# First batch's x through SP's hardware queue as fp32, in place of a casting load issued by POOL

## The chip, the cores and the metric

One core of one Trainium2 chip. The metric is the device time of one launch in microseconds (us). Runs are sorted into fast and slow by their time and by the clock that PE was granted.

Engines: PE multiplies matrices, DVE and ACT copy from PSUM (where PE leaves its results) to SBUF (where its operands lie), POOL and SP issue DMAs here. Sixteen DMA engines move the data between HBM, the memory outside the core, and SBUF. What POOL issues stands in the profile as the software queue, what SP issues as the hardware queue.

## The reference

```python
batch, m, k, n = 32, 512, 1024, 768
x      = randn(batch, m, k)  float32
weight = randn(batch, k, n)  float32
return np.matmul(x, weight)  # float32
```

A batch reads 2.10 MB of x and 3.15 MB of w and writes 1.57 MB of output, all as fp32 in HBM; 32 batches are 218 MB.

## The kernel before

Loads are issued by POOL and cast fp32 to bf16 on the way. PE transposes x as pairs of bf16 viewed as fp32 (so one fp32 transpose moves two bf16 columns), DVE copies the result out of PSUM, PE multiplies in bf16, ACT and DVE copy the sums to SBUF, and POOL issues the store.

```python
def load_x(b):
    xs[b] = x_pool.tile([P, MT, K], BF16, name="x_sb")
    nc.gpsimd.dma_start(out=xs[b], in_=x_view[b])       # POOL, casts

def load_w(b):
    ws[b] = w_pool.tile([P, KT, N], BF16, name="w_sb")
    ...                                                  # POOL, casts

def transpose(b, mt):
    pt = tpsum.tile([P, JT, P], F32, name="pt")
    pairs = xs[b].bitcast(F32)
    for j in range(JT):                                  # 4 transposes
        nc.tensor.transpose(pt[:, j, :], pairs[:, mt, j::JT], ident)
    xT = xT_pool.tile([P, JT, P, 2], BF16, name="xT")
    nc.vector.tensor_copy(...)                           # 1 copy
    return xT

load_x(0)
load_w(0)
ident = ...
for b in range(1, AHEAD):        # AHEAD = 3; x and w have 4 buffers each
    load_x(b)
    load_w(b)
for b in range(B):
    if b + AHEAD < B:
        load_x(b + AHEAD)
        load_w(b + AHEAD)
    if b > 0:
        nc.gpsimd.dma_start(out=out_view[b - 1], in_=outs[b - 1])
    ...                          # transposes, matmuls, evacuation
```

Of the kernel before, what the change touches and what calls it, by code (L numbers as in the profile page):

```python
# [1 line left out]

# [5 lines left out]

F32 = mybir.dt.float32
BF16 = mybir.dt.bfloat16  # L10


@with_exitstack
def kernel(
    ctx: ExitStack,
    tc: tile.TileContext,
    x: bass.AP,
    weight: bass.AP,
    out: bass.AP,
):  # L20
    nc = tc.nc
    B, M, K = x.shape
    _, _, N = weight.shape
    P = 128
    MT = M // P
    KT = K // P
    JT = KT // 2
    N2 = 2 * N
    CHUNKED = {B - 4: (4, 4), B - 3: (4, 4), B - 2: (4, 4), B - 1: (4, 2, 2)}
    AHEAD = 3  # L30

    const = ctx.enter_context(tc.tile_pool(name="const", bufs=1))
    w_pool = ctx.enter_context(tc.tile_pool(name="w", bufs=4))
    x_pool = ctx.enter_context(tc.tile_pool(name="x", bufs=4))
    xT_pool = ctx.enter_context(tc.tile_pool(name="xT", bufs=8))
    out_pool = ctx.enter_context(tc.tile_pool(name="out", bufs=7))
    tpsum = ctx.enter_context(tc.tile_pool(name="tpsum", bufs=2, space=bass.MemoryType.PSUM))
    mpsum = ctx.enter_context(tc.tile_pool(name="mpsum", bufs=2, space=bass.MemoryType.PSUM))



    w_view = weight.rearrange("b (ki ko) n -> b ki ko n", ki=P)
    x_view = x.rearrange("b (mi mo) k -> b mi mo k", mi=P)
    out_view = out.rearrange("b (mi mo) n -> b mi (mo n)", mi=P)

    xs, ws, outs = {}, {}, {}

    def banks():
        return [mpsum.tile([P, 512], F32, name=f"pm{i}") for i in range(3)]

    def load_x(b):
        xs[b] = x_pool.tile([P, MT, K], BF16, name="x_sb")
        nc.gpsimd.dma_start(out=xs[b], in_=x_view[b])  # L53

    def load_w(b):
        ws[b] = w_pool.tile([P, KT, N], BF16, name="w_sb")
        at = 0
        for n in CHUNKED.get(b, (KT,)):
            nc.gpsimd.dma_start(out=ws[b][:, at:at + n, :], in_=w_view[b, :, at:at + n, :])  # L59
            at += n  # L60
# [5 lines that stand above are left out]
        for j in range(JT):  # L66
            nc.tensor.transpose(pt[:, j, :], pairs[:, mt, j::JT], ident)  # L67
        xT = xT_pool.tile([P, JT, P, 2], BF16, name="xT")
        nc.vector.tensor_copy(  # L69
            xT.rearrange("p j m r -> p (j m r)"), pt.bitcast(BF16).rearrange("p j m -> p (j m)")  # L70
        )
        return xT



    SPLITS = (
        ((0, 0, 0, 512), (1, 0, 512, N - 512)),
        ((1, N - 512, 0, 1024 - N), (2, 0, 1024 - N, N2 - 1024)),
    )

    def matmuls(pm, half, xT, b, kos, together):
        for ko in kos:
            for i, (bank, at, off, size) in enumerate(SPLITS[half]):
                shares = half == 1 and i == 0
                nc.tensor.matmul(  # L85
                    pm[bank][:, at:at + size],
                    xT[:, ko // 2, :, ko % 2],
                    ws[b][:, ko, off:off + size],
                    start=(ko == 0 and not (together and shares)),
                    stop=(ko == KT - 1),  # L90
                    skip_group_check=together,
                )

    def evacuate(b, pair, pm):
        o = outs[b][:, pair * N2:(pair + 1) * N2]
        nc.scalar.copy(o[:, 0:512], pm[0])  # L96
        nc.vector.tensor_copy(o[:, 512:1024], pm[1])  # L97
        nc.scalar.copy(o[:, 1024:N2], pm[2])  # L98

    with tc.manual_schedule():  # L100
        load_x(0)
        load_w(0)
        ident = const.tile([P, P], F32)
        make_identity(nc, ident)
        for b in range(1, AHEAD):
            load_x(b)
            load_w(b)

        ready = {}
# [5 lines that stand above are left out]
                nc.gpsimd.dma_start(out=out_view[b - 1], in_=outs[b - 1])  # L115
            outs[b] = out_pool.tile([P, MT * N], F32, name="out_sb")
            if b not in CHUNKED:
                xT = {mt: transpose(b, mt) for mt in (0, 1)}
                for pair in range(2):
                    pm = banks()  # L120
                    for half in range(2):
                        if pair == 0:
                            matmuls(pm, half, xT[half], b, range(KT), False)
                            xT[2 + half] = transpose(b, 2 + half)
                        else:
                            matmuls(pm, half, xT[2 + half], b, range(KT), False)
                    evacuate(b, pair, pm)
                continue
            xT = ready.pop(b, None) or {mt: transpose(b, mt) for mt in range(MT)}
            pms = [banks() for _ in range(2)]  # L130
            at = 0
            for n in CHUNKED[b]:
                last = at + n == KT
                for mt in range(MT):
                    if last and b + 1 < B:
                        ready.setdefault(b + 1, {})[mt] = transpose(b + 1, mt)
                    matmuls(pms[mt // 2], mt % 2, xT[mt], b, range(at, at + n), True)
                    if last and mt % 2 == 1:
                        pair = mt // 2
                        evacuate(b, pair, pms[pair])  # L140
                        if b == B - 1:
                            cols = slice(pair * N2, (pair + 1) * N2)
                            nc.sync.dma_start(out_view[b, :, cols], outs[b][:, cols])
                at += n


# [1 line left out]
_INS = ['x', 'weight']  # L148
_OUTS = [((32, 512, 768), 'float32')]


# [23 lines left out]
```

## Time and profile before

| | before |
|---|---|
| time, first three runs, median | 518.48 us |
| span of the profiled execution | 516.5 us |
| PE, DVE, ACT busy | 82%, 25%, 15% |
| software DMA queue busy, of 16 engines' span | 99.9% |

The page of the kernel before: DMA busy tenths in 40 slices of the span, then the queues with packets, MB and busy share.

```profile
DMA  8999999999999999999999999999999999999996
q0 software_dynamic: 14400, 132.65, 99.9%
q1 hardware_dynamic: 288, 1.57, 0.7%
```

Only the first and the last of the 40 slices are not full (a 9 stands for 90% or more). What is to be saved in DMA time without moving fewer bytes lies, for the most part, there.

The timeline of POOL in the kernel before (start, length, engine, line, operation, output and input; in brackets the idle time ahead and what ended it), first the head, then one batch of the steady part:

```profile
1.26 0.67 POOL L53 DMA_DIRECT2D x_sb<-in_x_dram  x1 [0.81 <-POOLq L159]
1.93 0.55 POOL L59 DMA_DIRECT2D w_sb<-in_weight_dram  x1
...
25.44 0.53 POOL L53 DMA_DIRECT2D x_sb<-in_x_dram  x1 [19.23 <-PE pt L67]
30.64 0.53 POOL L59 DMA_DIRECT2D w_sb<-in_weight_dram  x1 [4.67 <-PE pm L85]
...
321.69 0.53 POOL L53 DMA_DIRECT2D x_sb<-in_x_dram  x1 [6.69 <-DMA w_sb<-in_weight_dram]
325.36 0.53 POOL L59 DMA_DIRECT2D w_sb<-in_weight_dram  x1 [3.14 <-DMA out_dram<-out_sb]
330.26 0.54 POOL L115 DMA_DIRECT2D out_dram<-out_sb  x1 [4.38 <-DMA x_sb<-in_x_dram]
337.47 0.53 POOL L53 DMA_DIRECT2D x_sb<-in_x_dram  x1 [6.67 <-DMA w_sb<-in_weight_dram]
```

In the steady part each issue waits until an earlier transfer has landed (the one eight places before), so the gaps between issues are the durations of transfers: an output lands 3.67 us after a w, an x 4.90 us after that, a w 7.21 us later. That is 428 to 436 GB/s each, counted in fp32 bytes, although x and w are written to SBUF as half as many bf16 bytes. A batch takes 15.78 us of DMA.

The timeline of PE in the kernel before, its first transposes and first matmuls, and two pieces of the chain that ended last (start, length, what), around the landing of the last x:

```profile
9.55 1.96 PE L67 MATMUL pt<-ident,x_sb 128*128 128x128 f32 x8 [9.55 <-DMA x_sb<-in_x_dram]
16.70 4.89 PE L85 MATMUL pm<-w_sb,xT 128*128 128x512 bf16 x16 [5.19 <-DMA w_sb<-in_weight_dram]
```

```profile
457.72 31.16 DMA x_sb<-in_x_dram
488.88 0.04 issue
```

### The profile page before, as it was taken

How to read it: one execution, taken by the hardware profiler on the slowest of the kernel's cores; microseconds unless marked ns; L12 is line 12 of the kernel's file. 1: busy time of each engine (PE TensorE's matmuls, PEld its weight loads, DVE VectorE, ACT ScalarE, POOL GpSimd, SP SyncE). 2: the span in 40 equal slices, each digit the busy share in tenths (PEclk: the TensorE clock that was granted, in tenths of full speed). 3: DMA queues.
4: the chain of work that ended last, by engine and by line, in shares of the span. 5: the costliest groups of instructions: out<-in, count | busy, mean ns of one | idle time of the engine just before them, and what ended most of it. 6: DMA issues, size and time to landing. Idle time of an engine off the chain costs nothing.

```text
span 516.5 us, 5888 instructions
## 1 busy us (share of the span) xinstructions
PE 424.2 (82%) x2512; PEld 277.7 (54%) x2560; DVE 127.0 (25%) x192; ACT 76.3 (15%) x129; POOL 53.9 (10%) x106
## 2 busy tenths in 40 slices
PE   1799999788887979868897879887887986978992
PEld 1466666455554656545564546554555653655561
DVE  1133333133131331322321213312223121322221
ACT  0011111111111111101110101111111110111111
POOL 3011010100101001100011010010100101111000
PEclk9999999899897998989998979998899897988997
DMA  8999999999999999999999999999999999999996
GB/s 158 217 218 216 211 274 278 272 268 240 263 274 275 278 249 246 279 275 274 266 233 270 278 275 271 245 256 278 273 276 255 245 273 272 276 266 242 256 387 265
DMA packets 14714, 134.60 MB, mean 261 GB/s; under 512 B 1632, under 2 KB 1632, under 8 KB 3040
## 3 DMA queue, kind: packets, MB, share of 16 engines
q0 software_dynamic: 14400, 132.65, 99.9%
q1 hardware_dynamic: 288, 1.57, 0.7%
q8 instruction: 20, 0.33, 0.2%
q14 instruction: 6, 0.05, 0.0%
HBM read 167.77 MB, written 50.33 MB: 422 GB/s over the span
## 4 chain that ended last, share of the span: by engine, by line
DMA 74%; PE 21%; DVE 2%; issue 1%; ACT 0%; POOL 0%; POOLq 0%
DMA w_sb<-in_weight_dram 37%; DMA out_dram<-out_sb 24%; PE pm L85 19%; DMA x_sb<-in_x_dram 13%; PE pt L67 2%; DVE xT L69 1%; DVE out_sb L97 1%; ACT out_sb L98 0%; POOL x_sb L53 0%; POOLq L53 0%; POOLq L59 0%; POOLq L159 0%
## 5 line engine op out<-in xcount | busy, mean ns | idle before, releaser
L85 PE MATMUL pm<-w_sb,xT 128*128 128x256 bf16 (+1 forms) x2000 | 370.7, 340 | 66.6 <-DMA w_sb<-in_weight_dram 61.9
L85 PEld LDWEIGHTS <-xT 128*128 128x128 bf16 x2048 | 207.2, 102 | 204.6 <-issue 72.9
L69 DVE COPY xT<-pt 128x1024 bf16<-128x1024 bf16 x128 | 85.8, 689 | 264.0 <-PE pt L67 264.0
L67 PE MATMUL pt<-ident,x_sb 128*128 128x128 f32 x512 | 80.3, 291 | 15.9 <-DMA x_sb<-in_x_dram 15.6
L67 PEld LDWEIGHTS pt<-ident,x_sb 128*128 128x128 f32 x512 | 76.3, 207 | 24.1 <-issue 14.6
L96 ACT COPY out_sb<-pm 128x512 f32<-128x512 f32 x64 | 37.5, 586 | 287.9 <-PE pm L85 284.5
L97 DVE COPY out_sb<-pm 128x512 f32<-128x512 f32 x64 | 43.9, 687 | 116.2 <-PE pm L85 116.2
L98 ACT COPY out_sb<-pm 128x512 f32<-128x512 f32 x64 | 37.5, 586 | 142.4 <-PE pm L85 142.2
L53 POOL DMA_DIRECT2D x_sb<-in_x_dram x32 | 17.1, 536 | 192.6 <-DMA w_sb<-in_weight_dram 141.8
L59 POOL DMA_DIRECT2D w_sb<-in_weight_dram x37 | 19.7, 532 | 114.2 <-DMA out_dram<-out_sb 56.5
L115 POOL DMA_DIRECT2D out_dram<-out_sb x31 | 16.6, 536 | 136.8 <-DMA x_sb<-in_x_dram 64.7
L96 ACT ACT_TABLE_LOAD x1 | 1.3, 1283 | 0.7 <-PEq L159 0.7
masks.py:199 POOL TENSOR_SCALAR_AFFINE_SELECT ident<-ident 128x128 f32<-128x128 f32 x1 | 0.3, 288 | 0.1
masks.py:197 POOL MEMSET ident<- 128x128 f32 x1 | 0.2, 243 | 0.0
L159 POOL MEMSET const-float32-0.0<- 128x1 f32 x1 | 0.1, 99 | 0.2 <-issue 0.2
L159 POOL MEMSET const-bfloat16-1.0<- 128x1 bf16 x1 | 0.1, 103 | 0.0
L159 POOL MEMSET const-uint8-127<- 128x1 uint8 x1 | 0.1, 103 | 0.0
L159 POOL MEMSET const-float32-1.0<- 128x1 f32 x1 | 0.1, 100 | 0.0
## 6 DMA issues: line engine op xcount, KB each, us to landing
out_dram<-out_sb POOLq DMA_DIRECT2D x31, 1536.0 KB, 41.9
w_sb<-in_weight_dram POOLq DMA_DIRECT2D x28, 1536.0 KB, 43.2
x_sb<-in_x_dram POOLq DMA_DIRECT2D x32, 1024.0 KB, 39.6
w_sb<-in_weight_dram POOLq DMA_DIRECT2D x7, 768.0 KB, 31.4
out_dram<-out_sb SPq DMA_DIRECT2D x2, 768.0 KB, 7.0
w_sb<-in_weight_dram POOLq DMA_DIRECT2D x2, 384.0 KB, 28.7
```

The lines of the kernel that those rows point to most:

```text
L53: nc.gpsimd.dma_start(out=xs[b], in_=x_view[b])
L59: nc.gpsimd.dma_start(out=ws[b][:, at:at + n, :], in_=w_view[b, :, at:at + n, :])
L67: nc.tensor.transpose(pt[:, j, :], pairs[:, mt, j::JT], ident)
L69: nc.vector.tensor_copy(xT.rearrange("p j m r -> p (j m r)"), pt.bitcast(BF16).rearrange("p j m -> p (j m)"))
L85: nc.tensor.matmul(pm[bank][:, at:at + size], xT[:, ko // 2, :, ko % 2], ws[b][:, ko, off:off + size], start=(ko == 0 and not (together an ...
L96: nc.scalar.copy(o[:, 0:512], pm[0])
L97: nc.vector.tensor_copy(o[:, 512:1024], pm[1])
L98: nc.scalar.copy(o[:, 1024:N2], pm[2])
L115: nc.gpsimd.dma_start(out=out_view[b - 1], in_=outs[b - 1])
L159: nc = _bacc.Bacc("TRN2", target_bir_lowering=False, num_devices=1)
```

## The change

The intent: SP stands idle at the start and can issue before POOL does. SP's load is written as a plain copy, so x of batch 0 arrives as fp32; each of its four row groups then needs eight fp32 transposes in place of four paired ones, and two DVE copies that also round to bf16.

```diff
+    first_pool = ctx.enter_context(tc.tile_pool(name="first", bufs=1))
...
+    def transpose_first(mt):
+        xT = xT_pool.tile([P, JT, P, 2], BF16, name="xT")
+        for h in range(2):
+            pt = tpsum.tile([P, JT, P], F32, name="pt")
+            for i in range(JT):
+                nc.tensor.transpose(pt[:, i, :], x_first[:, mt, JT * h + i::KT], ident)
+            nc.vector.tensor_copy(
+                xT[:, 2 * h:2 * h + 2].rearrange("p j m r -> p j r m"),
+                pt.rearrange("p (j r) m -> p j r m", r=2),
+            )
+        return xT
...
-        load_x(0)
+        x_first = first_pool.tile([P, MT, K], F32)
+        nc.sync.dma_start(x_first, x_view[0])
         load_w(0)
...
-                xT = {mt: transpose(b, mt) for mt in (0, 1)}
+                turn = transpose if b else lambda _, mt: transpose_first(mt)
+                xT = {mt: turn(b, mt) for mt in (0, 1)}
...
-                            xT[2 + half] = transpose(b, 2 + half)
+                            xT[2 + half] = turn(b, 2 + half)
```

## The prediction

> What bounds the kernel now. The DMA engines. The page's slices show DMA at 0.9 or more in all but the first and last, and its queue line shows the software queue busy 99.9% of the engines' span; PE is 82% busy, DVE 25%. After 86 us the chain of waits is almost all DMA. Before that it is PE, but with slack: eight loads (21 MB read) are queued by 6 us, and PE takes 12.8 us a batch against 15.8 us of DMA.
>
> What a transfer costs. In POOL's timeline, from about 59 us on, each issue follows the landing of the transfer eight places before, so the gaps between issues measure transfers: x 4.92 us, w 7.2, output 3.66, 15.8 a batch. Over the fp32 bytes (2.10, 3.15, 1.57 MB) all are 426 to 437 GB/s. The time goes with the fp32 side, not with the bf16 side that a cast writes. So x of batch 0 costs the same 4.9 us when written as fp32: the change takes no DMA work away and adds none.
>
> What it moves. POOL issues its first DMA at 1.26 us (0.67 us long); the first packet is recorded near 2.65 us. SP is free from 0.7 us. In the tail SP issued at 506.06 us and its first packets appear about 0.9 us later. My estimate from these: SP's first packets near 1.7 to 1.9 us, so the engines start 0.7 to 0.9 us earlier. The Trainium skill, "DMA: Bandwidth & Descriptors", section "Issuing engines are not separate DMA queues", says that all queues share the same 16 engines and a second issuer only saves issue time; the equal rates here fit. What is saved at the head moves the whole saturated queue, with it the landing of the last x (488.9 us) and the end. That is the whole gain: about 0.8 us of 518.
>
> What it adds, off the critical path. x and w of batch 0 share the engines: together still 5.24 MB, so w lands near 16 us (16.66 before), but x at about 14 us in place of 9.5. Sixteen fp32 transposes (245 ns each in the cold first group) and four copies of about 0.69 us (as the 128x512 fp32 eviction) then precede the matmuls: first matmul 17 to 18.5 us, before 16.70. Batch 0 has 16 more transposes (160 ns each, 2.6 us of PE) and 4 more DVE copies (2.8 us). PE is 2 to 4 us late with batch 0. It costs nothing: POOL's refills at 30.6 to 44 us come that much later, while the queued 21 MB last until about 50 us; the x load of batch 4 no longer waits for batch 0's transposes (issued near 6 us, was 25.4).
>
> Predicted time: 517.7 us, 516.7 to 518.6 in 8 of 10. Faster by over 2%: 0.01; within 2%: 0.98; slower: 0.01.
>
> What would show the steps right: first packets before 2 us on the hardware queue; x of batch 0 landing at 13 to 15.5 us; w within 1 us of 16.6; the x load of batch 4 issued by 7 us; POOL's steady gaps unchanged; the last x landing 0.5 to 1 us earlier; the tail after it still about 28 us.
>
> What would make it wrong: SP issuing no earlier than POOL (gain 0); the two queues disturbing each other so that the first 5.24 MB take longer than 12 us; a PE delay over 20 us that drains the queue; an order of issues that leaves the last loads later; a clock change in the tail, which is matmul-bound.

## More of the kernel before

The head in windows (length, then busy time of PE, its weight loads, DVE, ACT and POOL, then PE's granted clock, the DMA engines' busy share, GB/s written), kernel before:

```profile
0.00:2.00 2.00, 0.00 (x0) 0.00 (x0) 0.00 (x0) 1.25 (x1) 0.94 (x6) 1.00 0.00 0
2.00:4.00 2.00, 0.00 (x0) 0.00 (x0) 0.00 (x0) 0.03 (x1) 1.92 (x5) 1.00 0.83 86
```

And the DMA view of the first 20 us: all packets, then the software queue.

```profile
DMA packets 401, 3.55 MB, mean 177 GB/s; under 512 B 32, under 2 KB 32, under 8 KB 32
q0 software_dynamic: 401, 3.55, 88.9%
```

No byte moves in the first 2 us. These 3.55 MB are bf16, so 7.10 MB of fp32 were read; this sum, "fp32 MB by 20 us", is the measure of the head used below. At 430 GB/s 7.10 MB would take 16.5 us, so by this estimate about 3.5 us of the head go unused.

## The result

| | before | after |
|---|---|---|
| time, median of 6 runs each | 518.13 us | 517.64 us |
| range | 517.75 to 518.51 | 516.90 to 517.73 |
| ratio of the fast runs, 95% interval | | 0.9987, 0.9975 to 1.0 |
| span of the profiled execution | 516.5 us | 516.0 us |
| fp32 MB by 20 us | 7.10 | 7.56 |
| w of batch 0 landed | 16.63 us | 15.87 us |

A ratio is the mean time of one kernel's fast runs over the mean of the other's in the same rounds, so it is not quite the ratio of the medians.

The page of the changed kernel, its queues:

```profile
q0 software_dynamic: 14256, 131.60, 98.9%
q1 hardware_dynamic: 432, 3.67, 1.9%
```

The first 20 us of the changed kernel, DMA view:

```profile
DMA packets 434, 4.83 MB, mean 241 GB/s; under 512 B 41, under 2 KB 41, under 8 KB 41
q0 software_dynamic: 290, 2.73, 64.9%
q1 hardware_dynamic: 144, 2.10, 29.0%
```

The 2.10 MB on the hardware queue are fp32 as written; the 2.73 MB on the software queue stand for 5.46 MB. Together 7.56 MB, 0.46 MB more than before at the same moment. At 430 GB/s that is a lead of 1.07 us. (The page's own GB/s must not be used for this: it counts written bytes, and it rises merely because x is now written as fp32.)

The head of the changed kernel, windows:

```profile
0.00:2.00 2.00, 0.00 (x0) 0.00 (x0) 0.00 (x0) 1.26 (x1) 0.94 (x6) 1.00 0.46 90
2.00:4.00 2.00, 0.00 (x0) 0.00 (x0) 0.00 (x0) 0.02 (x1) 1.93 (x5) 1.00 0.63 205
```

The engines now work before 2 us, though they are not full yet (share 0.63 from 2 to 4 us); SP's first packets stand in the window from 1.6 to 1.8 us, where before the first was recorded at 2.6 to 2.7 us. The timeline of the changed kernel:

```profile
0.74 0.38 SPq L116 DMA_DIRECT2D x_first<-in_x_dram  x1
1.26 0.67 POOL L60 DMA_DIRECT2D w_sb<-in_weight_dram  x1 [0.81 <-POOLq L175]
...
5.61 0.59 POOL L54 DMA_DIRECT2D x_sb<-in_x_dram  x1
12.38 3.60 PE L81 MATMUL pt<-ident,x_first 128*128 128x128 f32 x16 [12.38 <-DMA x_first<-in_x_dram]
15.87 2.76 PE L99 MATMUL pm<-w_sb,xT 128*128 128x512 bf16 x16
...
28.51 0.53 POOL L60 DMA_DIRECT2D w_sb<-in_weight_dram  x1 [22.31 <-PE pm L99]
```

SP issues at 0.74 us and its x lands 11.5 us later, at 12.24. The x load of batch 4 is out at 5.61 us, 20 us earlier than before, but only behind seven others in a full queue. The refill of w comes at 28.51 us, 2.1 us earlier than before. In the chain the last x lands here, hardly moved:

```profile
457.90 31.18 DMA x_sb<-in_x_dram
489.08 0.04 issue
```

So the head gained 0.76 us (landing of w) to 1.07 us (bytes), this profiled execution is 0.5 us shorter, and yet the last x landed 0.20 us later than before. A single pair of traces does not close the account; the experiments do.

### The profile page after: what moved, and what is told of

Same layout as the page of the kernel before. It is cut to its first block, busy times and chain, and to the rows that moved or that the text cites. A ratio compares the mean times of both kernels' runs of the same rounds, so it can differ in the third digit from the quotient of the medians.

```text
span 516.0 us, 5924 instructions
## 1 busy us (share of the span) xinstructions
PE 426.4 (83%) x2528; PEld 279.6 (54%) x2576; DVE 129.7 (25%) x196; ACT 76.3 (15%) x129; POOL 53.4 (10%) x105
## 4 chain that ended last, share of the span: by engine, by line
DMA 88%; PE 9%; issue 1%; DVE 0%; ACT 0%; POOLq 0%
DMA x_sb<-in_x_dram 37%; DMA w_sb<-in_weight_dram 25%; DMA out_dram<-out_sb 24%; PE pm L99 7%; DMA x_first<-in_x_dram 2%; PE pt L81 1%; PE pt L68 1%; DVE out_sb L111 0%; DVE xT L70 0%; ACT out_sb L112 0%; POOLq L130 0%; POOLq L54 0%; POOLq L60 0%
## 5 line engine op out<-in xcount | busy, mean ns | idle before, releaser
L70 DVE COPY xT<-pt 128x1024 bf16<-128x1024 bf16 x124 | 83.0, 689 | 245.4 <-PE pt L68 245.4
L68 PE MATMUL pt<-ident,x_sb 128*128 128x128 f32 x496 | 77.4, 290 | 8.9 <-DMA x_sb<-in_x_dram 8.6
L68 PEld LDWEIGHTS pt<-ident,x_sb 128*128 128x128 f32 x496 | 73.7, 207 | 17.2 <-issue 7.1
L130 POOL DMA_DIRECT2D out_dram<-out_sb x31 | 16.6, 536 | 140.8 <-DMA x_sb<-in_x_dram 62.8
L81 PE MATMUL pt<-ident,x_first 128*128 128x128 f32 x32 | 5.7, 338 | 12.4 <-DMA x_first<-in_x_dram 12.4
L81 PEld LDWEIGHTS pt<-ident,x_first 128*128 128x128 f32 x32 | 4.9, 202 | 13.0 <-issue 12.3
L82 DVE CAST xT<-pt 128x512 bf16<-128x512 f32 x8 | 5.5, 727 | 18.4 <-PE pt L81 18.3
## 6 DMA issues: line engine op xcount, KB each, us to landing
x_first<-in_x_dram SPq DMA_DIRECT2D x1, 2048.0 KB, 11.5
```

The lines of the kernel that those rows point to most:

```text
L70: nc.vector.tensor_copy(xT.rearrange("p j m r -> p (j m r)"), pt.bitcast(BF16).rearrange("p j m -> p (j m)"))
L81: nc.tensor.transpose(pt[:, i, :], x_first[:, mt, JT * h + i::KT], ident)
L82: nc.vector.tensor_copy(xT[:, 2 * h:2 * h + 2].rearrange("p j m r -> p j r m"), pt.rearrange("p (j r) m -> p j r m", r=2),)
```

## The experiments

Theory A is the prediction's: the engines start about 0.8 us earlier, and because they are full from there to the end, that lead reaches the end. Its rivals: B, batch 0 is computed earlier, which frees buffers earlier; C, the half microsecond is scatter; D, a plain copy on the hardware queue is cheaper than a cast on the software queue. Each result gives the median, and the ratio to the kernel before with its 95% interval. Calls of several kernels shared one chip and nine runs of before.

### The change again, twice (no edit)

> The changed kernel unedited, for a second profile and more timed pairs. Theory A (the engines start earlier and the saturated queue carries that to the end): ratio to before 0.998 to 0.9995, w of batch 0 lands at 15.6 to 16.1 us (before 16.63, first profile of the change 15.87), about 0.4 to 0.5 MB (in fp32 bytes) more moved by 20 us than before. Theory C (the half microsecond is run to run scatter): ratio 1.000 within 0.001 and the head's lead no larger than what two profiles of one kernel differ by.

> The changed kernel unedited once more, beside the three below, so that they are compared with it on one chip. Theory A: ratio to before 0.9980 to 0.9993 as in the first two measurements (0.9987, 0.9993).

First repeat: 517.49 us, ratio 0.9993 (0.998 to 1.0005). Second: 517.00 us, ratio 0.9976 (0.9963 to 0.9988). The gains of the three measurements, as differences of means, are 0.65, 0.43 and 1.33 us; their average is 0.81 us. With the first repeat alone C would stand; the interval of the second excludes it. That ratio of 0.9976 lies below the range expected (0.9980 to 0.9993).

The head repeats itself closely: fp32 MB by 20 us are 7.62 and 7.56, w of batch 0 lands at 15.7 to 15.8 us. The last x landed at 488.2 us in both, 0.67 us before the profiled execution of before. The chain of the first repeat:

```profile
457.04 31.17 DMA x_sb<-in_x_dram
488.21 0.04 issue
```

The first profile of the change was thus an unlucky one, and that of before a lucky one, as the kernels of the experiments below show. In the four traces without an early start the last x landed at 488.88 (before), 489.25 (before with the tail edit), 489.23 (POOL's fp32 load) and 489.68 us (SP held back), on average 489.26. In the six with one, and POOL on time, it landed at 489.08, 488.21 and 488.22 (the change), 488.82 (batch 1), 487.88 and 488.50 us (both with the tail edit), on average 488.45: the lead is still 0.81 us at the last load. The times say the same: 31 runs of those with an early start average 517.35 us, 48 of those without 518.27, which is 0.92 us, with a standard error of 0.1. That excludes C.

Where the single traces part can be placed: POOL's steady issues are equally spaced again in all of them from about 160 us on, but for steps near 220 to 250 us and at 442 us, and the 0.9 us between the first profile of the change and its repeat arise between 60 and 115 us, where POOL's waits pass from PE to the DMAs. Why is open.

### SP's load held back

```diff
-        nc.sync.dma_start(x_first, x_view[0])
         load_w(0)
+        nc.gpsimd.memset(x_first[:, 0, 0:1], 0.0)   # SP must wait for this
+        nc.sync.dma_start(x_first, x_view[0])
```

> Only the start of SP's load is held back, behind a small write on POOL that follows the issue of w of batch 0; fp32 load, hardware queue, transposes and casts stay. Theory A: the lead is gone, first packet near 2.6 us from the software queue as before, w of batch 0 and x together done near 16.6 us, time 518.0 to 518.6, ratio 0.999 to 1.001. Theory D (a plain copy on the hardware queue is cheaper for the engines than a cast on the software queue): the lead stays, ratio about 0.9987 as in the change.

518.45 us, ratio 1.0008 (0.9994 to 1.0022): no gain is left, with the rest of the change in place but for the order (w of batch 0 is now issued first). The interval overlaps that of the change on the same chip (0.998 to 1.0005), so the lead in bytes decides, and it is gone. D falls: fp32, hardware queue and all, it is no cheaper. So does another rival, that POOL, with one load fewer, issues the rest one place earlier: here too it does (w of batch 0 at 1.26 us, before 1.93). DMA view of the first 20 us, this kernel:

```profile
q0 software_dynamic: 259, 2.52, 64.2%
q1 hardware_dynamic: 144, 2.10, 25.0%
```

2.10 MB and twice 2.52 MB are 7.14 MB; the kernel before has 7.10 and the change 7.56. The expectation missed one thing: x and w were not done together near 16.6 us. w landed at 15.2 and x only at 18.8 us. The timeline of this kernel:

```profile
2.07 0.38 SPq L118 DMA_DIRECT2D x_first<-in_x_dram  x1
...
18.90 3.50 PE L81 MATMUL pt<-ident,x_first 128*128 128x128 f32 x16 [18.90 <-DMA x_first<-in_x_dram]
22.24 2.76 PE L99 MATMUL pm<-w_sb,xT 128*128 128x512 bf16 x16
```

PE began its matmuls 5.5 us later than in the kernel before, and the time is 0.3 us above it, which the interval does not tell from nothing. So PE has slack of that order in the head. (That batch 0 came late is not what took the gain: with the early load of batch 1, below, it comes late too and the gain stays.)

### The fp32 load issued by POOL

```diff
-        nc.sync.dma_start(x_first, x_view[0])
+        nc.gpsimd.dma_start(out=x_first, in_=x_view[0])
```

> x of batch 0 is still loaded as fp32 and transposed as fp32, but issued by POOL at the place of the old load. Theory A: no lead; x lands near 9.5 us, w near 16.6 us, ratio 0.999 to 1.001. Theory D with the cast as the cheaper or dearer part: x lands more than 0.3 us earlier or later than the 9.5 us of before. Also: PE will sit idle about 3 us between the transposes and the first matmul; if the idle gap is what made the first 16 matmuls take 4.9 us in before and 2.8 us after the change, they take more than 2.8 us here.

518.24 us, ratio 1.0005 (0.9993 to 1.0018). x landed 8.1 us after its issue (8.2 with the cast, before), w at 16.66 us. fp32 MB by 20 us: 7.10, as before. A plain copy and a cast of the same fp32 source took the engines the same time. The gain belongs to SP's early issue, not to the type.

PE then waited for w, and this kernel's timeline shows what that costs:

```profile
16.66 4.19 PE L99 MATMUL pm<-w_sb,xT 128*128 128x512 bf16 x16 [3.50 <-DMA w_sb<-in_weight_dram]
```

The first 16 matmuls took 4.19 us after 3.50 us of idle time, 4.89 us after 5.19 us in the kernel before, and 2.76 us in the first two traces of the change, where the transposes run straight into them. In the second repeat, though, they took longer without any gap:

```profile
16.01 3.84 PE L99 MATMUL pm<-w_sb,xT 128*128 128x512 bf16 x16
```

Over all traces the first sixteen took 2.76 to 3.84 us without a gap and 4.19 to 5.28 us behind one of 3.5 us or more. This kernel has the same sixteen transposes as the change, so the gap is the likely cause that the matmuls behind it are slow; the 3.84 us show that it is not the only one. (In the kernel before only eight transposes precede the gap; that PE had not come up to speed there is possible too.)

### Another batch's x through SP

SP loads x of batch 1 at the start; batch 0 is loaded by POOL as before.

```diff
-        nc.sync.dma_start(x_first, x_view[0])
+        nc.sync.dma_start(x_first, x_view[1])
+        load_x(0)
...
-            load_x(b)
+            if b > 1:
+                load_x(b)
...
-                turn = transpose if b else lambda _, mt: transpose_first(mt)
+                turn = transpose if b != 1 else lambda _, mt: transpose_first(mt)
```

> SP loads x of batch 1 as fp32 at the start, in place of batch 0's; batch 0 is loaded by POOL with a cast as in before. Theory A: any bytes moved early count, so the lead in fp32 bytes by 20 us and the time are those of the change (ratio 0.998 to 0.9995), though x and w of batch 0 land 3 to 5 us later (w near 20 us) and PE starts later. Theory B (the gain is that batch 0 is computed earlier, which frees buffers and starts the refills earlier): no gain or a loss.

516.99 us, ratio 0.9980 (0.9968 to 0.9993), no slower than the change. x of batch 0 landed at 13.6 us and w at 20.8 us, both over 4 us later than before the change, so batch 0 was late. B falls: what batch the early bytes belong to does not matter, only that they move early. fp32 MB by 20 us are 2.10 and twice 2.78, 7.66:

```profile
q0 software_dynamic: 298, 2.78, 66.0%
q1 hardware_dynamic: 144, 2.10, 29.4%
```

### The effect enlarged: POOL late, with and without SP's load

Eight needless writes on POOL ahead of its first load, in the kernel before and in the changed one.

```diff
+        idle = const.tile([P, 512], F32)
+        for _ in range(8):
+            nc.gpsimd.memset(idle, 0.0)
         load_x(0)        # changed kernel: the SP load of x stands here
         load_w(0)
```

> The kernel before, with eight needless writes of a 128x512 fp32 tile on POOL ahead of its first load (about 4 to 8 us, read from the profile as D). Theory A: nothing makes up for a late start of the engines: the time grows by D, give or take 0.7 us. Rival: the slack of the first 50 us or the idle engines of the tail take up part of it, and the time grows by clearly less than D.

> The changed kernel with the same eight writes on POOL: SP's load fills the engines while POOL is late. Theory A: the 2.1 MB of x (about 4.9 us of all engines) are moved in the gap, so this kernel is faster than the one before with the same writes by 4 to 5.5 us if D is 5 us or more, else by about D + 0.8 us. Theory C or B: the difference stays near 0.5 us, since the start of the hardware queue does not matter.

| | first DMA of POOL | time, median | ratio to before |
|---|---|---|---|
| before, POOL late | 5.28 us (was 1.26) | 522.11 us | 1.008 (1.0065 to 1.0096) |
| after, POOL late | 5.28 us | 517.80 us | 0.9998 (0.9984 to 1.0011) |

The delay D is 4.02 us, and the kernel before became 3.94 us longer by the medians, 4.0 by the means: a late start is paid in full, at the end of a 518 us kernel. The timeline of POOL in this late kernel shows its first issue, and that the delay is still whole at 325 us (before: 321.69):

```profile
5.28 0.67 POOL L53 DMA_DIRECT2D x_sb<-in_x_dram  x1
...
325.70 0.53 POOL L53 DMA_DIRECT2D x_sb<-in_x_dram  x1 [6.69 <-DMA w_sb<-in_weight_dram]
```

With SP's load in front, the same delay is hidden, and the two kernels with it differ by 4.3 us. A expected about D + 0.8 = 4.8, since D is below 5 us, and so half a microsecond too much; C and B expected about 0.5. The software queue by 20 us, first in the late kernel before, then both queues of the late changed kernel:

```profile
q0 software_dynamic: 290, 2.70, 68.4%
```

```profile
q0 software_dynamic: 279, 2.65, 64.6%
q1 hardware_dynamic: 144, 2.10, 29.0%
```

In fp32 bytes these are 5.40 and 7.40 MB. At 430 GB/s the 1.70 MB that the first lacks against before are 4.0 us (3.94 measured), and the 2.00 MB between the two are 4.7 us (4.3 measured). The windows of the late changed kernel show why:

```profile
0.00:2.00 2.00, 0.00 (x0) 0.00 (x0) 0.00 (x0) 1.26 (x1) 1.35 (x7) 1.00 0.57 106
2.00:4.00 2.00, 0.00 (x0) 0.00 (x0) 0.00 (x0) 0.02 (x1) 1.83 (x4) 1.00 0.63 213
4.00:6.00 2.00, 0.00 (x0) 0.00 (x0) 0.00 (x0) 0.00 (x0) 1.89 (x5) 1.00 1.01 434
```

The engines carry x while POOL is busy with nothing. This pair is the clearest proof of A: the same cause as in the change, five times the size (4.3 against 0.81 us), and far outside the scatter.

### The price of the load

The kernel before, plus SP's fp32 load of x of batch 0 into a tile that nothing reads.

```diff
+        x_first = first_pool.tile([P, MT, K], F32)
+        nc.sync.dma_start(x_first, x_view[0])
         load_x(0)
         load_w(0)
```

> The kernel before, plus SP's fp32 load of x of batch 0 into a tile that nothing reads; results right. It prices the load and the early start in one: 2.10 MB at 426 to 431 GB/s are 4.9 us of all engines, of which about 0.8 us fall in the head that was idle before. Theory A: time up by 3.8 to 4.6 us. If the engines were not what bounds the kernel, or the plain copy were much cheaper than the cast: up by less than 3 us.

521.97 us, ratio 1.0074 (1.006 to 1.0087): 3.8 us longer. The load should take 4.9 us of full engines; 3.8 were paid, so about 1.1 us of it fell in time that was idle. That agrees with the lead of 1.07 us read from the bytes, and it shows once more that the engines bound the kernel: 2.10 useless MB in 218 cost their transfer time less what fell in the idle head. The bytes agree: by 20 us the software queue, which carries all that is used, had moved 5.46 MB (twice 2.73) in place of 7.10, and 1.64 MB at 430 GB/s are 3.8 us.

### The tail

In the first trace of the changed kernel the engines are not full near the end (506 to 509 us, share 0.43 to 0.60 in steps of 1 us). Traces differ in this: over the same stretch the share was 0.89 in the kernel before and 0.97 in the first repeat of the change. One edit tried to move the store of the first pair of output tiles there, by loading the last batch's w in two parts instead of three:

```diff
-    CHUNKED = {..., B - 1: (4, 2, 2)}
+    CHUNKED = {..., B - 1: (4, 4)}
```

It ran with the change, with the kernel before alone, and with the early load of batch 1.

> The changed kernel with the last batch's w in two loads of four rows instead of 4, 2, 2, so that the first pair of output tiles is complete about 6 us before the second and its store can run in the time in which the engines are not full (506 to 509 us). If the end is set by the stores that all come after the last matmuls: 0.5 to 2 us faster than the change. If the last rows of w now land later than PE wants them, or the engines were busy with the store of batch 30 anyway: no gain or a loss up to 1 us.

> The kernel before with the last batch's w in two loads of four rows and nothing else: what the tail edit is worth without the change. If head and tail add up: 0.4 to 0.8 us faster than before (the change with this edit was 517.02 us, the change without it 517.5 to 517.6 us on another chip). If the tail edit only worked together with the change: no gain.

> SP loads x of batch 1 as fp32 at the start, batch 0 as before, and the last batch's w in two loads of four rows. If the gains add up (head 0.5 to 1.1 us, tail 0.4 to 0.8 us): 1.0 to 1.8 us faster than before, 516.3 to 517.2 us, and the fastest of all. If the extra half microsecond that the early load of batch 1 showed against the early load of batch 0 was scatter: the same as the change with the tail edit, 517.0 us.

| | median | ratio to before |
|---|---|---|
| change and tail edit | 517.02 us | 0.9983 (0.9971 to 0.9996) |
| before and tail edit | 518.39 us | 1.0004 (0.9991 to 1.0016) |
| early batch 1 and tail edit | 517.30 us | 0.9988 (0.9974 to 1.0003) |
| change alone, same chip as the last two | 517.00 us | 0.9976 (0.9963 to 0.9988) |

The first looked like a gain of about half a microsecond on the change; the second shows no gain from the tail edit alone, and the third that nothing adds up. The half microsecond is within the scatter, and the expectation of 0.4 to 0.8 us from the tail was wrong. Nor does this chip bear out that the early load of batch 1 is better than that of batch 0. No version found beats the changed kernel.

## Why the prediction was right, and where it was not

- **The time.** Predicted 517.7 us (516.7 to 518.6), measured 517.64. The predicted gain was 0.8 us; the three measurements average 0.81, with single values from 0.43 to 1.33. That the average fits so closely is in part luck; that the gain has this size is not, since the lead at the last x is 0.81 us as well (six traces against four).
- **The engines bound the kernel and no DMA work goes away.** Shown: a late POOL costs 3.94 of its 4.02 us, 2.10 MB more cost 3.8 us, and the cast and the plain copy land alike (8.2 and 8.1 us after issue). The Trainium skill, "DMA: Bandwidth & Descriptors", section "Issuing engines are not separate DMA queues", on which the step rested, agrees: the second queue brought only the earlier issue.
- **SP's first packets at 1.7 to 1.9 us, 0.7 to 0.9 us earlier.** Right: 1.6 to 1.8 us, before 2.6 to 2.7; the lead was 0.76 us by the landing of w and 1.07 us by bytes. Holding SP back took the gain away.
- **x lands at about 14 us (13 to 15.5).** Wrong: 12.24 us. I let the two queues share evenly from the start. In the trace the software queue's first packet comes only at 5.3 to 5.6 us; till then the hardware queue has the engines alone, and about 1 MB of x has moved.
- **First matmul at 17 to 18.5 us, PE 2 to 4 us late with batch 0, refills later.** Wrong in sign: first matmul at 15.87 us, refill 2.1 us earlier (0.9 in the second repeat). Two terms failed: x landed earlier than reckoned, and I had not counted that PE without an idle gap runs the first 16 matmuls in 2.76 (3.84 in the second repeat) in place of 4.89 us. This more than paid for the added transposes. The error did no harm because the step's conclusion, slack, was right: with matmuls 5.5 us late, the held-back kernel was not clearly slower, and with matmuls 4.1 us late (20.83 us) the early load of batch 1 kept the gain.
- **x of batch 4 issued by 7 us, POOL's steady gaps unchanged.** Right: 5.61 us, and the steady issues of the change stand 3.66, 4.92 and 7.20 us apart.
- **Added work.** The eight rounding copies took 5.5 us in all where four plain ones took about 2.8 us (689 ns each): 2.7 us more, as predicted (2.8).
- **The last x 0.5 to 1 us earlier.** Not in the first profile (0.20 us later), but in both repeats (0.67 us earlier) and in the averages (0.81). A step of this size should not have been offered as a check on one trace.
- **A matmul-bound tail of about 28 us.** The length held (516.0 - 489.1 = 26.9 us, before 27.6), but "matmul-bound" is not supported: in the first profile of the change the last copies came 1.8 us later than before (508.57 against 506.74 us), and the span was still 0.5 us shorter, while the last stores landed in 5.3 us in place of 7.0. (1.6 of the 1.8 us arise between 489 and 495 us, where the chain has slower transposes and matmuls.) What sets the end exactly is open.

## What to carry to other kernels

When the DMA engines stay full from the head to the end, as here, an idle microsecond at the head costs about a microsecond at the end of the kernel; look for an engine that can issue earlier. Here it did not matter for which batch. The most that this can bring is the idle head itself: here, by the estimate above, about 3.5 us of 518, of which the change won about 1. If an effect is smaller than the scatter of runs, enlarge its cause on purpose (a late issuer, a doubled load) and read the lead in bytes moved by a fixed moment, which repeats to a few hundredths of a megabyte.

## What the Trainium skill lacked or had wrong

- "DMA: Bandwidth & Descriptors", section "Queues, rings and completion order", says that an engine takes turns between the queues it has work for, a packet at a time. At the start this was not seen: after SP's first packet (1.6 to 1.8 us) the software queue, issued at 1.26 us, shows none until 5.3 to 5.6 us; in the kernel with SP held back the roles are exchanged (software from 2.6 us, hardware, issued at 2.07, not before 6.1 us). The queue that comes first has the engines for 3.5 to 4 us; after that both move packets. The traces do not show why.
- No page that I read says what a casting load costs. Here it goes by the fp32 bytes read: in the steady part 2.10 MB of x take 4.9 us with the cast, and at the head x lands 8.2 us after its issue with the cast and 8.1 us as a plain copy.
- "DMA: Bandwidth & Descriptors", section "Where 436 GB/s comes from", lets about 358 GB/s bind transfers between HBM and SBUF. On a single core these runs do not agree: 428 to 436 GB/s in the steady part, 422 to 423 over the span. They agree with the 425 GB/s that the same section mentions as measured beside it.
- "TensorE: Matmul & The Clock Gate", section "Part 1: The HAM clock gate (the "warmup" mystery)", tells of a half clock after an idle window of about 3.4 us. The matmuls agree for the most part (16 in 4.19 us after 3.50 us idle, 4.89 after 5.19, 2.76 to 3.84 after none), and the granted clock of the kernel with POOL's fp32 load falls to 0.50 from 17 to 19 us. But in the kernel before that column stands at 1.00 from 16 to 20 us over equally slow matmuls (5 started in each us in both, 9 or 10 later). The page warns that clock events in traces have been seen to be unreliable; it does not name this case, a 1.00 at the head of a trace over such matmuls.
